# Reading the first 512 columns of an up projection in turns, and issuing compression products in pairs of groups

## The chip, the cores and the metric

The kernel runs on one core of a Trainium2 chip. The metric is device time of one execution in microseconds (us). Engines are named as the profile names them: PE is TensorE (products), PEld its weight loads, DVE is VectorE, ACT is ScalarE, POOL is GpSimd and SP is SyncE, whose queue issues nearly all loads.

## The reference

One layer of a hybrid decoder, for 256 tokens of width 2048, in float32. Cut to what matters here:

```python
def compress_blocks(k, pe, w1, w2):        # keys and values of attention's compressed branch
    ...                                    # 15 overlapping blocks of 32 tokens, each 32*128 long
    return jax.nn.gelu(flat @ w1) @ w2     # w1: 4096 x 256, once for keys, once for values

def conv_ffn(h, w_up, conv_w, conv_b, w_down):
    a, g = jnp.split(h @ w_up, 2, axis=-1) # w_up: 2048 x 11264
    a = causal_dwconv(a, conv_w, conv_b)
    return (jax.nn.silu(a) * g) @ w_down

# per layer
mod = (c_act @ w_ada[l] + b_ada[l])        # w_ada: 2048 x 12288, six vectors
h = layer_norm(x) * (1.0 + sc1) + sh1
y = token_mixer(h, w_in[l], ...)           # w_in: attention, mLSTM and merge gates
x = layer_norm(ALPHA * x + g1 * y, ...)
h = layer_norm(x) * (1.0 + sc2) + sh2
y = conv_ffn(h, w_up[l], ...)
x = layer_norm(ALPHA * x + g2 * y, ...)
```

## The kernel before

**Precision.** Most products are made in the reduced type fp32r (the profile writes f32 for it too). A weight tile `w` is split into a high part `wh` (a cast on ScalarE, L147) and a low part `wl` (a subtraction on VectorE, L150), and the activations likewise; three products (high-high, high-low, low-high) stand for one float32 product. A few small products stay native float32: these show as two instructions (passes) each.

**Reading in turns.** Where weights are the moving operand, `turns` (L111) lets the product read its columns as two halves alternately: column 0, column 256, column 1, column 257 and so on. The host has put the even columns into the first half and the odd ones into the second (`_even_odd`), so that the result has its old order. All projections with moving weights do so, but the first 512 columns of the up projection.

**Loading.** `load` (L121) takes a buffer of the pool `w` (seven of 512 KB) and issues a load on SP's queue, in the order of the program. `load_split` (L141) splits the tile; `wh` and `wl` have four buffers each. A `w` buffer comes free when its tile is split, or, for a tile that is used as it is, when its products are done.

**The input projection and the compression.** The input projection runs over three groups of k tiles. In the last group it goes through 21 tiles of `w_in_b` (products `ps_b`, 256 columns), then 14 of `w_in_a` (`ps_a`, 392 columns, four column blocks of 3.5 tiles), then 7 of `w_in_v`. `stream` calls `work()` once for every such tile. `work()` normally ticks the ticker `tk`, which at rate 1.0 issues one half row of `w_ada` (a 512 KB load and, one tick later, a VectorE product, L269). The compression starts when the thirteenth of the 21 `w_in_b` tiles has been gone through; it is a generator, and while it lasts `work()` only moves it on:

```python
if comp and next(comp[0], 1) is None:
    return
comp.clear()
```

`compress` (L593) makes for the keys, then for the values: `xe` (the blocks with their position term, L599 and L604; one buffer for both), eight groups of products `ps_hid` (L611), and behind them a copy `hp` (L616), four small products `ps_hs` (L619) and a Gelu. One group loads one 512 KB tile of `cmp_w1` and makes four native products of 32 columns by 256, in four column strips of the array. The scheduler places them on TensorE where they are ready.

**The first 512 columns of the up projection.** Columns 0 to 255 of both halves of `w_up` are handled apart, while the normalisation ahead of the feed-forward runs, in an order written out by hand (L1427 on, `manual_schedule`). Here the weights are the moving operand, 512 columns, into `acc` (`ps_u`). `turn2` transposes four k tiles of one half of the tokens (`ps_n`), `modulated` scales and shifts them, `high_part` and `low_part` split them into `h2T`. For the first half of the tokens and k tiles 0 to 11, `exact` (L1385) makes native products straight from the unsplit tile `raws`, 12 in all; `products` (L1415) makes the other 60 in fp32r from tiles that `early_split` has split. The results are transposed in `up(0)` and `up(1)`.

Of the kernel before, what the change touches and what calls it, by code (L numbers as in the profile page):

```python
# [14 lines left out]
P = 128  # L15
# [7 lines left out]
DFF = 5632  # L23
# [57 lines left out]
def build(ctx: ExitStack, tc: tile.TileContext, d, out, dbg=None):  # L81
# [26 lines left out]
    def mm(o, lhsT, rhs, start, stop):  # L108
        nc.tensor.matmul(o, lhsT, rhs, start=start, stop=stop)  # L109
# [483 lines left out]
    def compress():  # L593
        gTs = []
        w2t = t2([P, 2, 2, P], "w2t")
        nc.sync.dma_start(w2t, d["cmp_w2"].rearrange("p (a b c) -> p a b c", a=2, b=2))
        for kv in range(2):
            xe = pa.tile([P, 32, 2, 16], F32, name="xe", tag="xe")
            nc.gpsimd.memset(xe, 0.0)  # L599
            ch = accC[:, 2 * kv:2 * kv + 2, :].rearrange("p g (n q) -> p q g n", q=16)  # L600
            for a in range(2):
                pe = prm[:, R_PE + 32 * kv + 16 * a:R_PE + 32 * kv + 16 * a + 16]
                for g in range(2):
                    nc.vector.tensor_tensor(xe[:, 16 * a:16 * a + 16, g, 0:NCMP],  # L604
                                            ch[:, :, g, a:a + NCMP],
                                            pe[:, :, None].to_broadcast([P, 16, NCMP]), op=ALU.add)
            ps = bank(psa, "ps_hid")
            for i in range(8):
                t = load(d["cmp_w1"][kv * 8 + i])
                for l in range(4):  # L610
                    mm(ps[32 * l:32 * l + 32, :256],  # L611
                       xe[:, 4 * i + l, :, :].rearrange("p g n -> p (g n)"),
                       t[:, l * 256:(l + 1) * 256], i == 0, i == 7)
                yield
            hp = t2([P, 256], "hp")
            nc.vector.tensor_copy(hp, ps[:, :256])  # L616
            ps = bank(psa, "ps_hs")
            for ho in range(2):
                mm(ps[:, ho * 32:(ho + 1) * 32], hp[:, ho * P:(ho + 1) * P], sel4, True, True)  # L619
            if kv:  # L620
                gt = t2([P, 4, 3, 16], "gT1")
                nc.scalar.activation(gt, ps[:, :64].rearrange("p (a n) -> p a n", a=4)[:, :, None, :]
                                     .to_broadcast([P, 4, 3, 16]), AF.Gelu_apprx_tanh)
            else:
                gt = pa.tile([P, 2, 32], F32, name="gT0")
                nc.scalar.activation(gt, ps[:, :64].rearrange("p (a b) -> p a b", a=2), AF.Gelu_apprx_tanh)
            gTs.append(gt)
        ps = bank(psa, "ps_kc")
        for ho in range(2):
            mm(ps[:, :32], w2t[:, 0, ho, :], gTs[0][:, ho, :], ho == 0, ho == 1)  # L630
        nc.vector.tensor_copy(kcT[:, :, :16], ps[:, :32].rearrange("p (a b) -> p a b", a=2))
        ps = bank(psa, "ps_vc")
        for g in range(2):
            for ho in range(2):
                mm(ps[:48, g * P:(g + 1) * P],
                   gTs[1][:, 2 * ho + g].rearrange("p a n -> p (a n)"), w2t[:, 1, ho, :],
                   ho == 0, ho == 1)
        src = ps[:48, :2 * P].rearrange("p (a b) -> p a b", a=2)
        nc.scalar.copy(vcm, src)
        nc.vector.tensor_sub(vcm[32:48], src[32:48], vcm[32:48])  # L640
# [131 lines left out]
    for gi, kn in enumerate(GROUPS):  # L772
# [16 lines left out]
        c = 0  # L789
# [594 lines left out]

    def exact(q, t, i):  # L1385
        k = 4 * q + i
        mm(acc[t], tmps[q, t][:, i, :], raws[k // 2][:, k % 2 * 512:(k % 2 + 1) * 512], k == 0, False)

    def turn2(q, t):
        psn[q, t] = bank(psa, "ps_n2")  # L1390
# [23 lines left out]

    def products(q, t, lo, ks=range(4)):  # L1415
        for k in [4 * q + i for i in ks]:
            wh, wl = [w[:, k % 2 * 512:(k % 2 + 1) * 512] for w in ews[k // 2]]
            x = h2T[:, k, lo, t * P:(t + 1) * P]
            if lo:
                mm(acc[t], x, wh, False, k == KD - 1)  # L1420
            else:
                mm(acc[t], x, wh, k == 0, False)
                mm(acc[t], x, wl, False, False)
# [265 lines left out]
def pack(inputs):  # L1689
    import numpy as np  # L1690
    f = {k: np.asarray(v) for k, v in inputs.items()}
    r = {}
    r["x"] = np.ascontiguousarray(f["x"][0])

    i = np.arange(P)
    e = np.zeros((P, R_HEAD), np.float32)
    e[:, R_ID:R_ID + P] = np.eye(P)
    e[:, R_C:R_C + KD] = f["c"][0].reshape(KD, P).T
    e[:, R_BADA:R_BADA + 96] = f["b_ada"][0].reshape(96, P).T
    r["head"] = e  # L1700
    c = q = np.zeros((P, R_N), np.float32)
    c[:, C_U:C_U + P] = i[:, None] <= i[None, :]
    c[:, C_ONE:C_ONE + 8] = 1.0
    r["msk"] = np.where(i[None, :] > i[:, None], NEG, 0.0).astype(np.float32)
    n = np.arange(16)
    for t in range(2):
        ok = (CMP_STRIDE * n[None, :] + CMP_LEN - 1 <= (t * P + i)[:, None]) & (n[None, :] < NCMP)
        c[:, C_CADD + 16 * t:C_CADD + 16 * t + 16] = np.where(ok, 0.0, NEG)
        c[:, C_C01 + 16 * t:C_C01 + 16 * t + 16] = ok
    c[:, C_SEL:C_SEL + 32] = (i % 32)[:, None] == np.arange(32)[None, :]  # L1710
    q[:, R_CW:R_CW + 32] = f["ml_conv_w"][0].reshape(4, 8, P).transpose(2, 1, 0).reshape(P, 32)
    q[:, R_CB:R_CB + 8] = f["ml_conv_b"][0].reshape(8, P).T
    fc = np.zeros((P, R_FN), np.float32)
    fc[:, :R_FB] = f["ffn_conv_w"][0].reshape(3, KF, P).transpose(2, 1, 0).reshape(P, 3 * KF)
    fc[:, R_FB:] = f["ffn_conv_b"][0].reshape(KF, P).T
    r["ffn"] = fc
    q[:, R_PE:R_PE + 64] = f["cmp_pe"][0].transpose(2, 0, 1).reshape(P, 64)
    q[:, R_NG:R_NG + 8] = f["ml_norm_g"][0].reshape(8, P).T
    r["prm"] = q
    r["ml_gate_b"] = f["ml_gate_b"]  # L1720
    r["ln_g"] = f["ln_g"][0]
    r["ln_b"] = f["ln_b"][0]

    wa = np.ascontiguousarray(f["w_ada"][0].T).reshape(6 * KD, P, 2, 1024)
    r["w_ada"] = np.ascontiguousarray(wa.transpose(0, 2, 1, 3)).reshape(12 * KD, P, 1024)

    w = f["w_in"][0]
    kv = lambda br, k, g: w[:, 1024 + ((br * 2 + k) * 2 + g) * P:1024 + ((br * 2 + k) * 2 + g + 1) * P]
    bc = [kv(0, 0, 0), kv(0, 0, 1), kv(0, 1, 0), kv(0, 1, 1),
          kv(1, 0, 0), kv(2, 0, 0), kv(1, 0, 1), kv(2, 0, 1), w[:, :1024], w[:, 2584:3608]]  # L1730
    bc = np.concatenate(bc, 1)
    ac = np.concatenate([w[:, 4640:5664], w[:, 2560:2584], w[:, 4632:4640], kv(1, 1, 0), kv(1, 1, 1),
                         kv(2, 1, 0), kv(2, 1, 1), w[:, 3608:4632]], 1)
    tb, ta, tv = [], [], []
    k0 = 0
    for gi, kn in enumerate(GROUPS):
        rows = slice(k0 * P, (k0 + kn) * P)
        u = bc[rows].reshape(kn, P, NBLK, P)
        u = np.stack([u[k, :, b, :] for b, ks in order_b(gi) for k in ks]).reshape(-1, 8, P, P)
        tb.append(np.ascontiguousarray(u.transpose(0, 2, 1, 3)).reshape(-1, P, 1024))  # L1740
        ta.append(_pack_u(_even_odd(ac[rows, :A_MV], AW), AW, 2))
        tv.append(_pack_u(_even_odd(ac[rows, A_MV:], 512), 512, 2))
        k0 += kn
    r["w_in_b"] = np.concatenate(tb)
    r["w_in_a"] = np.concatenate(ta)
    r["w_in_v"] = np.concatenate(tv)
    mg = [_pack_a(_even_odd(m, 512), 512).reshape(4, 8, P, 1024) for m in (w[:, 5664:7712], w[:, 7712:])]
    r["w_mg"] = np.stack(mg, 1).reshape(64, P, 1024)
    br = [_pack_a(_even_odd(f[m][0], 512), 512).reshape(4, 4, P, 1024) for m in ("w_br_nsa", "w_br_ml")]
    r["w_br"] = np.stack(br, 1).reshape(32, P, 1024)  # L1750
    r["w_o"] = _pack_rows(f["w_o"][0])
    up = f["w_up"][0]
    r["w_up"] = np.stack([_pack_b(up[:, :DFF], 8), _pack_b(up[:, DFF:], 8)], 1).reshape(KF * 4, P, 1024)
    r["w_up"][:8] = _pack_a(np.concatenate([up[:, c:c + 2 * P] for c in (0, DFF)], 1), 512)
    dn = f["w_down"][0]
    r["w_down"] = np.concatenate([_pack_a(_even_odd(dn[:DFF // 2], 512), 512), _pack_rows(dn[DFF // 2:])])
    w1 = f["cmp_w1"][0].reshape(2, 8, 4, P, 256)
    r["cmp_w1"] = w1.transpose(0, 1, 3, 2, 4).reshape(16, P, 1024)
    r["cmp_w2"] = f["cmp_w2"][0].reshape(2, 2, P, P).transpose(2, 0, 1, 3).reshape(P, 512)
    return {k: np.ascontiguousarray(v) for k, v in r.items()}  # L1760
# [20 lines left out]
```

## Time and profile before

| What | us |
|---|---|
| Runs: median of 3 (lowest, highest) | 1375.86 (1375.83, 1376.8) |
| The profiled execution | 1377.45 |
| Its span, first to last instruction | 1375.4 |
| TensorE busy | 1356.4 |
| VectorE busy | 1089.1 |
| ScalarE busy | 733.5 |

Busy time is a union of overlapping instructions: a product's duration contains the filling of the pipeline, and the next one starts before it ends. The work that a product costs TensorE is read from the distance between two starts. In a timeline row the first number is the start and the second the time from the first instruction's start to the last one's end, both in us; x is how many instructions of one kind follow each other; the brackets at the end hold idle time before it and what ended it. The mean granted clock of TensorE over the span is 0.997.

### The profile page before, as it was taken

Reading aid. Unit: us, or ns where it says so; the run is one execution under the profiler, and the core shown is the slowest. Engines: PE = TensorE matmul, PEld = TensorE weight load, DVE = VectorE, ACT = ScalarE, POOL = GpSimd, SP = SyncE. Lnnn points to the kernel's source line nnn. Section 1 sums busy time; section 2 is a strip of 40 time slices with the busy share of each in tenths; the row PEclk is TensorE's granted clock in tenths of the full one; section 3 lists DMA queues with packets and bytes.
Section 4 is the critical chain, followed back from the end, with each engine's and each line's share of the span. In section 5 each row is a group of like instructions: output and inputs, shape, how many; then the busy total and the mean of one; then the engine's idle time right before and its main releaser. Section 6 shows DMA issues by size and latency. Waiting matters only on the chain.

```text
span 1375.4 us, 20986 instructions
## 1 busy us (share of the span) xinstructions
PE 1356.4 (99%) x7890; PEld 1208.5 (88%) x7890; DVE 1089.1 (79%) x1643; ACT 733.5 (53%) x1053; POOL 3.6 (0%) x11
## 2 busy tenths in 40 slices
PE   7999999999999999999999999999999999999998
PEld 6999998888778888889689999988889999998887
DVE  7899977888787998789889889855557676765568
ACT  6644455646576444445665565553445555555342
POOL 0000000000000000000000000000000000000000
PEclk9999999999999999999999999999999999999999
DMA  9999978996877999996389878866676666666662
GB/s 372 418 419 365 393 258 280 350 314 230 323 255 273 381 339 359 362 343 250 119 323 310 296 251 301 293 197 206 198 205 201 202 203 202 200 200 200 205 201 84
DMA packets 103302, 374.09 MB, mean 272 GB/s; under 512 B 11168, under 2 KB 11680, under 8 KB 102432
## 3 DMA queue, kind: packets, MB, share of 16 engines
q1 hardware_dynamic: 103200, 372.75, 78.0%
q8 instruction: 62, 1.02, 0.3%
q14 instruction: 40, 0.33, 0.1%
HBM read 370.61 MB, written 2.10 MB: 271 GB/s over the span
## 4 chain that ended last, share of the span: by engine, by line
PE 85%; DVE 8%; DMA 2%; issue 2%; ACT 2%; SPq 0%; DVEq 0%; ACTq 0%
PE ps_up L109 32%; PE ps_d L109 14%; PE ps_mg L109 12%; PE ps_b L109 7%; PE ps_br L109 6%; PE ps_a L109 5%; PE ps_o L109 3%; DVE wl L150 3%; PE ps_u L109 2%; DVE adaA L251 1%; DMA w<-in_w_in_b_dram 1%; PE ps_s L109 1%; PE ps_y L109 1%; DVE adaB L251 1%; PE ps_hid L109 1%
## 5 line engine op out<-in xcount | busy, mean ns | idle before, releaser
L150 DVE TENSOR_TENSOR wl<-w,wh 128x1024 fp32r<-128x1024 f32 (+1 forms) x470 | 564.3, 1205 | 248.3 <-ACT wh L147 245.0
L147 ACT CAST wh<-w 128x1024 fp32r<-128x1024 f32 (+1 forms) x470 | 484.4, 1035 | 513.2 <-PE ps_up L109 145.0
L109 PE MATMUL ps_up<-h2T,wh 128*128 128x512 f32 x1344 | 440.6, 382 | 0.0
L109 PE MATMUL ps_up<-h2T,wl 128*128 128x256 f32 x1344 | 366.3, 273 | 0.0
L109 PEld LDWEIGHTS ps_up<-h2T,wh 128*128 128x128 f32 x1344 | 253.9, 189 | 35.4
L109 PEld LDWEIGHTS ps_up<-h2T,wl 128*128 128x128 f32 x1344 | 258.0, 192 | 0.1
L109 PE MATMUL ps_d<-wh,uTt 128*128 128x512 f32 (+1 forms) x704 | 198.5, 366 | 0.0
L109 PE MATMUL ps_mg<-wh,hT 128*128 128x512 f32 x512 | 163.1, 389 | 0.0
L269 DVE SCALAR_TENSOR_TENSOR w<-w,crow 128x1024 f32<-128x1024 f32 x132 | 160.7, 1218 | 0.0
L109 PEld LDWEIGHTS ps_d<-wh,uTt 128*128 128x128 f32 x704 | 129.8, 189 | 16.5
L109 PE MATMUL ps_b<-hT,wh 128*128 128x256 f32 x768 | 125.8, 278 | 3.5 <-ACT hT L429 2.5
L109 PE MATMUL ps_d<-wl,uTt 128*128 128x512 f32 (+1 forms) x352 | 128.8, 366 | 0.0
L109 PEld LDWEIGHTS ps_b<-hT,wh 128*128 128x128 f32 x768 | 111.7, 193 | 7.4 <-ACT hT L429 3.2
L109 PEld LDWEIGHTS ps_mg<-wh,hT 128*128 128x128 f32 x512 | 96.8, 189 | 16.0 <-issue 3.1
L109 PE MATMUL ps_a<-wh,hT 128*128 128x392 f32 (+1 forms) x384 | 103.5, 348 | 0.0
L109 PE MATMUL ps_mg<-wl,hT 128*128 128x512 f32 x256 | 97.2, 380 | 0.0
L109 PE MATMUL ps_b<-hT,wl 128*128 128x256 f32 x384 | 91.5, 278 | 0.0
L109 PEld LDWEIGHTS ps_a<-wh,hT 128*128 128x128 f32 x384 | 69.4, 189 | 5.4 <-issue 2.2
L109 PEld LDWEIGHTS ps_d<-wl,uTt 128*128 128x128 f32 x352 | 66.7, 189 | 8.3
L109 PEld LDWEIGHTS ps_b<-hT,wl 128*128 128x128 f32 x384 | 68.4, 195 | 0.1
L109 PE MATMUL ps_a<-wl,hT 128*128 128x392 f32 (+1 forms) x192 | 67.0, 350 | 1.3 <-DVE wl L150 1.2
L109 PE MATMUL ps_o<-wh,mgT 128*128 128x512 f32 x192 | 57.4, 379 | 0.0
(323 smaller groups left out, 1414.7 us busy)
## 6 DMA issues: line engine op xcount, KB each, us to landing
w<-in_w_up_dram SPq DMA_DIRECT2D x176, 512.0 KB, 4.3
w<-in_w_ada_dram SPq DMA_DIRECT2D x132, 512.0 KB, 5.0
w<-in_w_down_dram SPq DMA_DIRECT2D x89, 512.0 KB, 4.2
w<-in_w_mg_dram SPq DMA_DIRECT2D x64, 512.0 KB, 5.1
w<-in_w_in_b_dram SPq DMA_DIRECT2D x48, 512.0 KB, 9.8
w<-in_w_br_dram SPq DMA_DIRECT2D x32, 512.0 KB, 5.3
w<-in_w_o_dram SPq DMA_DIRECT2D x32, 512.0 KB, 5.1
adaA<-in_w_ada_dram SPq DMA_DIRECT2D x15, 1024.0 KB, 10.2
```

The source lines that it names most:

```text
L109: nc.tensor.matmul(o, lhsT, rhs, start=start, stop=stop)
L147: hi = nc.scalar.copy(wh[:, :n], t[:, :n])
L150: lows.append(nc.vector.tensor_sub(wl[:, :n], t[:, :n], wh[:, :n]))
L251: ins = nc.vector.scalar_tensor_tensor(t, t, 1.0, crow, op0=ALU.mult, op1=ALU.mult, accum_out=parts[:, row(m), k, 0:1])
L269: ins = nc.vector.scalar_tensor_tensor(t, t, 1.0, crow[:, i * 1024:(i + 1) * 1024], op0=ALU.mult, op1=ALU.mult, accum_out=parts[:, row(m), ...
```

## The change

Three places. `compress` yields after every second group instead of after each, so that two groups are issued in a row and one call of `work()` moves it on by two. `exact` and `products` read their moving operand through `turns`. The host stores the first 512 columns (the first eight tiles of `w_up`) with even columns first, then odd ones.

```diff
@@ compress
                     mm(ps[32 * l:32 * l + 32, :256],
                        xe[:, 4 * i + l, :, :].rearrange("p g n -> p (g n)"),
                        t[:, l * 256:(l + 1) * 256], i == 0, i == 7)
-                yield
+                if i % 2:
+                    yield
@@ exact
-        mm(acc[t], tmps[q, t][:, i, :], raws[k // 2][:, k % 2 * 512:(k % 2 + 1) * 512], k == 0, False)
+        mm(acc[t], tmps[q, t][:, i, :], turns(raws[k // 2][:, k % 2 * 512:(k % 2 + 1) * 512]),
+           k == 0, False)
@@ products
-            wh, wl = [w[:, k % 2 * 512:(k % 2 + 1) * 512] for w in ews[k // 2]]
+            wh, wl = [turns(w[:, k % 2 * 512:(k % 2 + 1) * 512]) for w in ews[k // 2]]
@@ pack
-    r["w_up"][:8] = _pack_a(np.concatenate([up[:, c:c + 2 * P] for c in (0, DFF)], 1), 512)
+    r["w_up"][:8] = _pack_a(_even_odd(np.concatenate([up[:, c:c + 2 * P] for c in (0, DFF)], 1), 512), 512)
```

## The prediction

> **What bounds the kernel now.** I read the page first, then who waited for whom on TensorE, then busy time by stretch around the two edits, then single rows of the timelines.
>
> ```profile
> span 1375.4 us, 20986 instructions
> ```
>
> ```profile
> PE ps_a L109 <- DVE wl L150: 1.2, 3, 0.7
> ```
>
> All that TensorE waits for split weight tiles in the projections beside the compression is 1.2 us in three times (the columns: us in total, times, longest). What counts is then the distance from one product's start to the next, since durations overlap, and whether the next weight tile goes on being split in time. By stretch (columns: busy of PE, PEld, DVE, ACT, POOL, clock, DMA share, GB/s):
>
> ```profile
> 190.00:200.00 10.00, 10.00 (x95) 9.79 (x98) 7.19 (x11) 5.69 (x8) 0.00 (x0) 1.00 0.74 249
> 200.00:210.00 10.00, 10.00 (x104) 8.75 (x94) 7.08 (x10) 3.77 (x5) 0.00 (x0) 1.00 0.84 321
> 210.00:220.00 10.00, 10.00 (x96) 8.46 (x95) 8.17 (x15) 6.93 (x12) 0.00 (x0) 1.00 0.89 299
> 220.00:230.00 10.00, 10.00 (x75) 9.47 (x74) 9.92 (x20) 4.78 (x9) 0.96 (x1) 1.00 0.68 212
> 230.00:240.00 10.00, 10.00 (x94) 7.42 (x94) 4.19 (x7) 4.67 (x7) 0.00 (x0) 1.00 0.80 284
> 240.00:250.00 10.00, 10.00 (x72) 9.04 (x65) 7.15 (x12) 3.79 (x5) 0.41 (x1) 1.00 0.99 379
> 250.00:260.00 10.00, 10.00 (x72) 8.77 (x71) 7.85 (x16) 8.79 (x12) 0.00 (x0) 1.00 0.98 368
> ```
>
> From 190 to 250 us, where the compression runs, TensorE has full clock and no gap; DMA and VectorE have room until 240, none and little after it.
>
> **Part 1, compression products two groups in a row.** No instruction is added or removed. One group is four native products of 32 columns, eight passes. TensorE's timeline, first a run of three, then a single group:
>
> ```profile
> 199.43 0.28 PE L109 MATMUL ps_b<-hT,wl 128*128 128x256 f32 x1
> 199.64 1.50 PE L109 MATMUL ps_hid<-w,xe 128*32 128x256 f32 x24
> 201.07 0.49 PE L109 MATMUL ps_b<-hT,wh 128*128 128x256 f32 x2
> 201.40 0.28 PE L109 MATMUL ps_b<-hT,wl 128*128 128x256 f32 x1
> ```
>
> ```profile
> 206.42 0.28 PE L109 MATMUL ps_b<-hT,wl 128*128 128x256 f32 x1
> 206.63 0.64 PE L109 MATMUL ps_hid<-w,xe 128*32 128x256 f32 x8
> 207.19 0.49 PE L109 MATMUL ps_b<-hT,wh 128*128 128x256 f32 x2
> 207.52 0.28 PE L109 MATMUL ps_b<-hT,wl 128*128 128x256 f32 x1
> 207.63 0.39 PE L109 MATMUL ps_b<-hT,wh 128*128 128x256 f32 x2
> ```
>
> Undisturbed products of 256 columns start 0.11 us apart (207.52 to 207.63). The single group pushes the third product behind it to 207.52 where 206.42 + 0.33 = 206.75 would do: 0.77 us. The run of three costs 201.40 - 199.43 - 0.33 = 1.64 us. So a further group in a run costs (1.64 - 0.77) / 2 = 0.435 us, and each change into and out of the 32-column form 0.77 - 0.435 = 0.335 us. The runs of before begin at 199.64, 206.63, 210.07, 213.51, 216.96 and 220.40 for the keys, and 230.85 (four groups), 234.24, 236.99, 239.75 and 242.50 for the values: 11 runs. The first two stand above; the first and the last of the values' five:
>
> ```profile
> 230.85 1.93 PE L109 MATMUL ps_hid<-w,xe 128*32 128x256 f32 x32
> ...
> 242.50 0.64 PE L109 MATMUL ps_hid<-w,xe 128*32 128x256 f32 x8
> ```
>
> After it, eight pairs. The two first runs were already long since xe came late; late again, it joins two pairs each time, which leaves three runs for each half, 6 in all (bounds: 8 with no joining, 4 if all is late). Gain 5 x 0.335 = **1.7 us**, between 1.0 and 2.3, as long as TensorE stays fed.
>
> What the pairs move is the larger question. work() calls the generator once for each weight tile and skips the ticks while it lasts. Half the yields end it eight tiles earlier: all sixteen groups now lie beside the eight last w_in_b tiles, and the eleven a tiles of columns 0 to 2 each bring one 512 KB w_ada load and its VectorE product, where three did. On SP's queue each of the eight last w_in_b loads stands behind two cmp_w1 loads instead of one, in the same seven w buffers, which cmp_w1 tiles hold until their group has run. Cost, by row:
>
> ```profile
> 20.00:100.00 80.00, 76.27 (x587) 73.75 (x587) 70.22 (x73) 48.09 (x73) 0.00 (x0) 0.98 1.03 419
> 214.39 0.97 DVE L150 TENSOR_TENSOR wl<-w,wh 128x784 fp32r<-128x784 f32 x1 [1.13 <-ACT wh L147]
> 223.75 0.33 PE L109 MATMUL ps_a<-wh,hT 128*128 128x392 f32 x1
> 231.55 1.28 ACT L626 ACT_TABLE_LOAD   x1
> 245.06 0.98 DVE L150 TENSOR_TENSOR wl<-w,wh 128x784 fp32r<-128x784 f32 x1 [1.59 <-ACT wh L147]
> 245.95 1.22 DVE L269 SCALAR_TENSOR_TENSOR w<-w,crow 128x1024 f32<-128x1024 f32 x1
> 246.99 0.49 PE L109 MATMUL ps_a<-wh,hT 128*128 128x392 f32 x2
> ```
>
> - DMA: eight 512 KB loads come forward into 190 to 250 us, 8 x 1.25 = 10.0 us at 419 GB/s or 11.1 at 379. The six stretches leave 10 x (0.26 + 0.16 + 0.11 + 0.32 + 0.20 + 0.01) = 10.6 us idle. It fits, barely, if all of it can be used.
> - VectorE: 8 x 1.2 = 9.6 us more, against 60 - 43.7 = 16.3 us idle there. It fits.
> - The lead of the splits over TensorE: the first a tile is split at 215.36 and used at 223.75, 8.4 us later; the tenth, counted by splits of 784 columns (245.06 to 246.04), is used at 247.16, the second product of the row at 246.99: 1.1 us. An a tile takes 12 products of 0.166 us, 2.0 us, while it and a w_ada tile (0.926 MB) need 2.4 us at 379 GB/s.
> - ScalarE: the keys' Gelu now falls among the convolution's Silu, one or two more table loads of 1.28 us; ScalarE is at most 69% busy there, and the splits' lead hides them (without it, 1.3 us once).
>
> If tiles come when they came, TensorE arrives 1.7 us sooner at a tile that was 1.1 us ahead, and waits 0.6 us. Bounds: 0, when the idle DMA time is all used, and 5.8 us (rival A). I take **0.6 us**, as the stretch from 250 to 260 us runs at a DMA share of 0.98 with w_ada loads in it, and TensorE does not stop there.
>
> Later the w_ada queue ends some eight loads sooner; nothing on TensorE waits for it there, so no gain.
>
> **Part 2, the first 512 columns.** 60 products in fp32r and 12 native ones (24 passes) read their 512 columns as two halves in turns; the permutation is on the host. Contiguous against turned:
>
> ```profile
> L109 PE MATMUL ps_u<-w,hm x24: 592/592/697, 666.2 to 677.5; 128*128 128x512 f32 x24
> 669.30 6.17 PE L109 MATMUL ps_u<-w,hm 128*128 128x512 f32 x14
> 675.95 1.50 ACT L1404 ACTIVATE hm<-ps_n,modc 128x128 f32<-128x128 f32 x4 [1.06 <-PE ps_n L1393]
> 680.75 1.37 DVE L1402 TENSOR_SCALAR hm<-ps_n,modc 128x128 f32<-128x128 f32 x4 [0.87 <-PE ps_n L1393]
> 686.80 1.22 DVE L150 TENSOR_TENSOR wl<-w,wh 128x1024 fp32r<-128x1024 f32 x1
> 688.07 0.50 PE L109 MATMUL ps_u<-wl,h2T 128*128 128x512 f32 x1
> 688.40 0.39 PE L109 MATMUL ps_u<-wh,h2T 128*128 128x512 f32 x1
> ...
> 691.39 0.39 PE L109 MATMUL ps_u<-wl,h2T 128*128 128x512 f32 x1
> ```
>
> ```profile
> 1000.42 0.38 PE L109 MATMUL ps_d<-wl,uTt 128*128 128x512 f32 x1
> ...
> 1003.66 0.38 PE L109 MATMUL ps_d<-wl,uTt 128*128 128x512 f32 x1
> ```
>
> 13 steps from 688.40 to 691.39 are 0.230 us each; the down projection's turned products make 15 steps in 3.24 us, 0.216. So 0.014 us each, 0.84 us for 60. Not all shows: the product at 688.07 starts when VectorE has finished wl (686.80 + 1.22 = 688.02). VectorE is then in one unbroken row from 680.75, which began with the transposes behind the first eight products. Of the 36 before 688 I count those eight, 0.11 us; the 24 after it count in full, 0.34. Together **0.45 us**; bounds 0.34 and 0.84.
>
> The native passes start (6.17 - 0.592) / 13 = 0.429 us apart, twice the turned fp32r step for as many columns, so the reading isn't what they wait for: 0 gained. No row shows a native product reading in turns. Its bounds are -0.36 us (24 x 0.015, what fp32r gains) and +10.3 us (every pass doubled). I take 0, as a turned read already feeds 512 columns in 0.216 us. [...]
>
> **Sum.** -1.7 + 0.6 - 0.45 = -1.55 us. The profiled execution took 1377.45 us (span 1375.4 and 2.05 around it), which would become 1375.9. It stands 1.6 us above the median of the runs, 1375.86; from the median, **1374.3 us**, 0.11% less. What a measurement of this kernel can tell from no change is about 0.2%, 2.75 us, so I forecast no difference that can be told.
>
> **Rivals.**
> A. The a tiles starve (slower). Place: the fifth to the eleventh a tile. Mechanism: cmp_w1 tiles fill the w buffers while xe is rebuilt for the values, and SP stands still behind them, as 220 to 230 us shows (share 0.68); then a tile and w_ada load in turns give a tile every 2.4 us where 2.0 is wanted. If half of the 10.6 us idle stays idle, 5.2 us of the 10.5 don't fit; with 1.1 us of lead and TensorE 1.7 us earlier, the wait is 5.2 - 1.1 + 1.7 = 5.8 us: 1375.86 - 2.15 + 5.8 = 1379.5. The time passes that of before once over 1.5 us don't fit, and is slower by over 0.2% from 4.3 us on. Against it: 1.1 us of lead at the worst tile, and 8.4 us of lead at the first. Chance 0.18.
> B. Everything comes in: four runs, 60 steps, no waiting: -2.3 - 0.84 = -3.1, 1372.7. Against it are the wait at 688.07 and the lead of 1.1. Chance 0.17 that it reaches 2.75.
> C. The grouping does little: pairs aren't joined, 8 runs, and what is saved is waited for later: -1.0 + 0.6 - 0.45, 1375.0. No change that can be told. Chance 0.15.
> D. Native products slow down when read in turns. These 24 passes lie on the chain (ScalarE stood idle 1.06 us until the transposes behind them, row at 675.95), so all of it shows; it cancels the rest from 1.55 / 24 = 0.065 us a pass on, and at half a pass, 0.215, the time is 1375.86 - 1.55 + 5.2 = 1379.5. Chance 0.04. [...]
>
> The forecast itself has 0.46. Faster by over 0.2%: 0.17 (B). Slower: 0.20 (most of A, D). Same: the forecast, C and the rest, 0.63. The range is from B's 1372.7 to 1379.0, short of A's and D's ends; the likeliest case alone lies within 1373.5 and 1375.2.
>
> **What would show it.** ps_hid in six runs on TensorE, none a single group of 8, the last before the first ps_a product; ps_u steps of 0.216 in fp32r and 0.429 native; w_ada loads beside every a tile. Wrong: waits of ps_a for wl summing over 3 us, or ps_u<-w,hm durations above 592.

## The result, and the profile after

The changed kernel is slower: 1383.88 us median of six runs (1381.85 to 1384.95), beside 1376.76 of the kernel before on the same chip (1375.83 to 1378.92, six runs). The ratio is 1.0051, 95% interval 1.0041 to 1.006. The profiled execution took 1384.77 us. Both parts of the change cost time, each in a place that the prediction had named as a rival.

Three views of the changed kernel show it. First the span and who waited for whom on TensorE (us in total, times, longest us):

```profile
span 1383.0 us, 20993 instructions
```

```profile
PE ps_a L109 <- DVE wl L150: 3.8, 7, 0.9
...
PE ps_a L109 <- ACT wh L147: 1.4, 2, 1.0
```

5.2 us in nine waits for split tiles over the whole span. Four of them, 1.5 us, lie ahead of 190 us; so do the three of before, 1.2 us, of which none lies beside the compression. The other five, 3.6 us, are new and stand between 241 and 265 us. By stretch, in the columns that the prediction named (busy time of PE, PEld, DVE, ACT, POOL, clock, DMA share, GB/s):

```profile
240.00:250.00 10.00, 8.56 (x50) 7.80 (x49) 9.97 (x16) 3.92 (x6) 0.00 (x0) 1.00 0.95 319
250.00:260.00 10.00, 9.06 (x54) 8.47 (x53) 8.81 (x17) 6.76 (x8) 0.00 (x0) 1.00 1.02 401
260.00:270.00 10.00, 8.79 (x46) 7.52 (x45) 8.10 (x14) 8.09 (x10) 0.00 (x0) 1.00 0.88 313
```

TensorE, without a gap there before, is now idle for 3.6 us in these three stretches. In the first two VectorE and the DMA queues are close to full.

Where the time goes, read from single tiles: each row gives the least, median and longest duration in ns, then the first and the last start in us. First the kernel before, then the changed one:

```profile
L109 PE MATMUL ps_hid<-w,xe x128: 379/379/403, 199.6 to 242.8; 128*32 128x256 f32 x128
L109 PE MATMUL ps_mg<-wl,hT x256: 378/379/462, 280.0 to 566.5; 128*128 128x512 f32 x128
L109 PE MATMUL ps_u<-wh,h2T x40: 387/390/497, 678.2 to 693.4; 128*128 128x512 f32 x40
```

```profile
L109 PE MATMUL ps_hid<-w,xe x128: 379/379/403, 198.5 to 226.4; 128*32 128x256 f32 x128
L109 PE MATMUL ps_mg<-wl,hT x256: 378/379/463, 284.1 to 570.6; 128*128 128x512 f32 x128
L109 PE MATMUL ps_u<-w,hm x24: 701/703/1122, 671.0 to 685.4; 128*128 128x512 f32 x24
L109 PE MATMUL ps_u<-wh,h2T x40: 379/379/562, 685.8 to 700.7; 128*128 128x512 f32 x40
```

From the first compression product to the first mixing gate (ps_mg) it took 280.0 - 199.6 = 80.4 us, and now 284.1 - 198.5 = 85.6: 5.2 us more. Three ps_b products that stood ahead of the first compression product now stand behind it (172 of them against 169), 0.3 us, so that 4.9 us are lost. The compression is over 16 us sooner. The mixing gates take as long as before. From the first to the last native ps_u product it took 11.3 us (the row of before stands in the prediction) and now 14.4: 3.1 lost. From there to the last fp32r product of wh it took 15.9, and now 15.3: 0.6 won.

The native passes by their timeline, the run of 14 that took 6.17 us before, with the transposes ahead of it:

```profile
669.26 1.92 PE L1395 MATMUL ps_n<-head,n 128*128 128x128 f32 x8 [1.90 <-ACT n L1373]
670.97 4.11 PE L109 MATMUL ps_u<-w,hm 128*128 128x512 f32 x6
674.92 0.60 PE L1395 MATMUL ps_n<-head,n 128*128 128x128 f32 x4
675.36 7.72 PE L109 MATMUL ps_u<-w,hm 128*128 128x512 f32 x14
```

(7.72 - 0.703) / 13 = 0.540 us a pass, where a pass read straight took 0.429: 0.111 more, times 23 steps 2.6 us. The other 0.5 us of the 3.1 are in the six passes from 670.97, where TensorE's granted clock was halved for a while:

```profile
669.36:672.78 3.42, 3.42 (x11) 2.24 (x12) 3.30 (x7) 2.97 (x8) 0.00 (x0) 0.50 0.00 0
```

And what VectorE does while TensorE waits for the a tiles, one row per run of instructions:

```profile
241.40 0.96 DVE L150 TENSOR_TENSOR wl<-w,wh 128x784 fp32r<-128x784 f32 x1
242.28 1.22 DVE L269 SCALAR_TENSOR_TENSOR w<-w,crow 128x1024 f32<-128x1024 f32 x1
243.43 0.09 DVE L269 DVE_READ_ACCUMULATOR w<-w,crow 128x1 f32 x1
243.43 0.97 DVE L150 TENSOR_TENSOR wl<-w,wh 128x784 fp32r<-128x784 f32 x1
...
247.49 1.04 DVE L863 TENSOR_TENSOR projA<-ps_a,projA 128x392 f32<-128x392 f32 x2
...
255.67 0.97 DVE L150 TENSOR_TENSOR wl<-w,wh 128x784 fp32r<-128x784 f32 x1
```

Split, w_ada product, split, w_ada product, an addition to projA after some three tiles, VectorE busy for 14.17 of 14.27 us: six tiles from 241.40 to 255.67, 2.38 us a tile. TensorE needs 12 x 0.166 = 2.0 us for one. That looks like a bound by VectorE; the experiments had to tell it from one by the DMA queue, which was the prediction's rival A.

The last of the five waits, 1.0 us at 264 us, ends with a cast on ScalarE instead. ScalarE had no idle time ahead of it: the gates' activations with three table loads (1.28 us each) stood there from 256.10 on, with one cast among them. The last of them and the cast:

```profile
261.72 1.28 ACT L687 ACT_TABLE_LOAD   x1
...
263.13 2.92 ACT L147 CAST wh<-w 128x1024 fp32r<-128x1024 f32 x3
```

In the kernel before, the same activations run with three table loads, but the first tile of this kind (1024 columns) is split by 258.19 and used from 260.62 on, and TensorE does not wait. No run changes this one alone.

### The profile page after: what moved, and what is told of

The parts are those of the page before. It is cut to its first block, busy times and chain, and to the rows that moved or that the text cites. A ratio compares the mean times of both kernels' runs of the same rounds, so it can differ in the third digit from the quotient of the medians.

```text
span 1383.0 us, 20993 instructions
## 1 busy us (share of the span) xinstructions
PE 1359.8 (98%) x7890; PEld 1209.3 (87%) x7890; DVE 1089.4 (79%) x1643; ACT 737.0 (53%) x1055; POOL 3.6 (0%) x11
## 4 chain that ended last, share of the span: by engine, by line
PE 82%; DVE 9%; DMA 4%; issue 2%; ACT 2%; SPq 0%; DVEq 0%; ACTq 0%
PE ps_up L109 32%; PE ps_d L109 14%; PE ps_mg L109 12%; PE ps_br L109 6%; PE ps_b L109 6%; PE ps_a L109 4%; PE ps_o L109 3%; DVE wl L150 3%; PE ps_u L109 2%; DMA w<-in_w_in_a_dram 1%; DMA w<-in_w_o_dram 1%; PE ps_s L109 1%; PE ps_y L109 1%; DMA w<-in_w_in_b_dram 1%; ACT wh L147 1%
## 5 line engine op out<-in xcount | busy, mean ns | idle before, releaser
L109 PE MATMUL ps_d<-wh,uTt 128*128 128x512 f32 (+1 forms) x704 | 198.5, 366 | 0.0
```

## The experiments

The kernel before was run again beside each set of experiments. Its median is 1377.21 us for the second part alone, the first part alone, the w_ada tiles held back and straight native reading; 1376.88 for products in pairs with loads one by one and the two kernels built on it; 1376.74 for short products, short loads, the lowered rate and the changed kernel once more. Ratios have their 95% interval.

**The second part alone** (`exact` and `products` in turns, `compress` as before).

> The kernel before with the second edit alone (the first 512 columns of the up projection read in turns, native and fp32r products), compression as before. Theory: the 24 native passes start 0.540 us apart instead of 0.429, 24 x 0.111 = 2.7 us, and the fp32r products give back 0.45 us: slower by 2.2 us, 1378.1 from a median of 1375.86; ps_u<-w,hm durations above 700 as in the changed kernel. Rival: the native passes are slow in the changed kernel only because TensorE's granted clock fell to 0.5 from 669 to 673 us in its profile; then, without that drop, they are at 592 again and the time is 0.45 us below before.

Measured: 1378.89 us, ratio 1.0014 (1.0005 to 1.0023), 1.7 us more than before. Its native products:

```profile
L109 PE MATMUL ps_u<-w,hm x24: 701/703/802, 665.2 to 679.0; 128*128 128x512 f32 x24
L109 PE MATMUL ps_u<-wh,h2T x40: 379/379/562, 679.3 to 694.3; 128*128 128x512 f32 x40
```

13.8 us for the native stretch instead of 11.3, 2.5 more, and 15.3 for the fp32r stretch instead of 15.9. TensorE's granted clock is 1.00 there, from 664 to 685 us, so the rival falls: the slow passes belong to the reading. +2.5 - 0.6 is 1.9, near the 1.7 measured.

**The first part alone** (the edit in `compress`).

> The kernel before with the first edit alone (compression products two groups in a row), the up projection as before. Theory: the a tiles starve: TensorE waits for split weights between 240 and 262 us, and every milestone from the mixing gates on is 4.1 us later; slower by 4.1 us, 1380.0, with 10 runs of compression products. Rival: the up projection's loads and the late stages share in the loss, so that the pairs alone cost under 2 us.

Measured: 1380.84 us, ratio 1.003 (1.0018 to 1.0042), 3.6 us more. Waits and milestones:

```profile
PE ps_a L109 <- DVE wl L150: 3.4, 6, 0.8
...
PE ps_a L109 <- ACT wh L147: 1.7, 2, 1.0
```

```profile
L109 PE MATMUL ps_mg<-wl,hT x256: 378/379/462, 283.9 to 570.5; 128*128 128x512 f32 x128
```

The loss stands there whole before the mixing gates begin (283.9 - 198.5 = 85.4 us from the first compression product, for 80.4), and the rival (a share lost in late stages) falls. About 1.2 us of it comes back at the last layer norm, where TensorE waited 0.5 us for `n` (the normalised rows) instead of 1.7; the changed kernel's first profile waited 1.9.

**The first part, with the w_ada tiles held back.**

```diff
         def work():
             if comp and next(comp[0], 1) is None:
                 return
+            if comp:
+                held_back[0] = 9
             comp.clear()
+            held_back[0] -= 1
+            if held_back[0] > 0:
+                return
```

> The kernel before with the first edit alone, but after the compression has ended the eight next calls bring no w_ada tile, so that the w_ada loads stand where they stood in the kernel before. Theory one (a w_ada load beside every a tile takes the DMA time that the a tiles need): the waits of ps_a go back to about 1 us, and the time is that of before less one change of form, 1375.5. Theory two (the compression's loads, two by two in front of each w_in_b load, eat the lead before the a tiles begin): the waits of ps_a stay above 3 us, and the time is 2 to 4 us above before, 1378 to 1380.

Measured: 1376.73 us, ratio 0.9995 (0.9986 to 1.0004). The waits are those of before, none of them beside the a tiles:

```profile
PE ps_a L109 <- DVE wl L150: 1.2, 3, 0.7
```

Theory two falls. The loads of the compression two by two do no harm; it is the w_ada work, brought forward to stand beside every a tile.

**Is it VectorE or the DMA queue?** Two kernels, each the first part alone, ease one of the two for the w_ada tiles beside the a tiles (`beside` is true from the end of the compression to the end of the third column block; the lines that set it are left out here). Neither computes the gates in full.

```diff
-            def products(t=t, i=i):
+            def products(t=t, i=i, n=128 if beside[0] else 1024):
                 ins = nc.vector.scalar_tensor_tensor(
-                    t, t, 1.0, crow[:, i * 1024:(i + 1) * 1024], ...
+                    t[:, :n], t[:, :n], 1.0, crow[:, i * 1024:i * 1024 + n], ...
```

> Pairs alone, and the VectorE products of the w_ada tiles that come beside the a tiles take 128 of their 1024 columns (the sums over the rest are left out, so the gates are not computed in full); their loads stay whole. Theory one (VectorE sets the pace: per three a tiles three splits, three w_ada products and the additions to projA, 7.1 us against the 6.0 us that TensorE needs): the products fall from 1.22 to about 0.2 us, VectorE keeps up, the waits of ps_a go back to about 1 us and the loss of 4.1 us goes, to about before or a little below it, 1375 to 1376. Theory two (the DMA queue sets it, a load of 512 KB and one of 392 KB per a tile): the waits stay above 3 us and the time at 1379 to 1381.

```diff
+            n = 64 if beside[0] else 1024
-            t = load(d["w_ada"][(m * KD + k) * 2 + i])
+            t = load(d["w_ada"][(m * KD + k) * 2 + i][:, :n])
...
+                if n < 1024:
+                    a, cr = [x[:, :1024][:, n:].rearrange("p (r n) -> p r n", n=n) for x in (t, cr)]
+                    b = t[:, :n][:, None, :].to_broadcast([P, 15, n])
...
```

> Pairs alone, and of the w_ada tiles that come beside the a tiles only 64 of 1024 columns are loaded (32 KB instead of 512); their VectorE products run over the 64 columns 15 times, so that VectorE works as long as before (the gates are not computed from the right numbers). Theory one (VectorE sets the pace): nothing changes, waits of ps_a above 3 us and 1379 to 1381. Theory two (the DMA queue sets it): the waits go and the time is about that of before.

Measured: short products 1380.58 us, ratio 1.003 (1.0019 to 1.0041); short loads 1379.01, ratio 1.0013 (1.0004 to 1.0022). Neither theory holds alone. The stretch from 230 to 260 us, first with short products, then with short loads:

```profile
230.00:260.00 30.00, 28.03 (x171) 24.75 (x170) 19.16 (x51) 18.44 (x25) 0.00 (x0) 1.00 0.96 348
```

```profile
230.00:260.00 30.00, 29.03 (x184) 26.80 (x182) 29.91 (x51) 15.30 (x21) 0.00 (x0) 1.00 0.68 203
```

With short products VectorE is free for 10.8 of 30 us and the DMA queues stay at a share of 0.96. The splits now wait for ScalarE's casts (the bracket), and four of the casts between 241 and 254 us for loads of `w_in_a`, 5.8 us in all. The first of these casts, then the first and the last of six splits:

```profile
242.65 0.84 ACT L147 CAST wh<-w 128x784 fp32r<-128x784 f32 x1 [1.33 <-DMA w<-in_w_in_a_dram]
```

```profile
241.36 0.98 DVE L150 TENSOR_TENSOR wl<-w,wh 128x784 fp32r<-128x784 f32 x1 [0.83 <-ACT wh L147]
...
254.29 0.96 DVE L150 TENSOR_TENSOR wl<-w,wh 128x784 fp32r<-128x784 f32 x1
```

That is five tiles in 12.9 us, 2.6 us each; 0.926 MB at 348 GB/s are 2.7 us. With short loads the DMA share falls to 0.68 and VectorE has no idle time left, 29.91 of 30; seven tiles from 242.20 to 258.34 take it 2.3 us each. So both are short at nearly the same height, 2.3 us and 2.6 us a tile against TensorE's 2.0, and easing one finds the other. By the medians, easing the loads gave back 1.4 of the 3.6 us (the two intervals overlap) and easing VectorE nothing.

**Both eased, with every w_ada product kept**: the first part alone, and the ticker's rate beside the a tiles lowered.

```diff
-GR1, GR2 = 1.0, 0.5
+GR1, GR2 = 0.6, 0.5
```

> Pairs alone, the planner's rate beside the a tiles at 0.6 instead of 1.0, so that six or seven of the eleven a tiles bring a w_ada tile; the rest comes later, in the mixing gates. Theory one: per three a tiles VectorE has 1.8 products in place of 3, 5.6 us, under TensorE's 6.0: most of the loss goes, within 0.5 us of before, with waits of ps_a of 1 to 2 us. Rival: any w_ada load beside the a tiles costs its share, 0.6 of the 4.1 us stay, 1378.3.

Measured: 1376.81 us, ratio 1.0000 (0.9992 to 1.0009).

```profile
PE ps_a L109 <- DVE wl L150: 1.2, 3, 0.7
```

By the times the whole loss is gone with eight w_ada products instead of eleven between 229 and 260 us, and TensorE has no idle time left beside the a tiles (busy for 30.00 of the 30 us from 230 on); the rival, a share for every load, falls.

The time of a kernel also holds the wait for `n` at the last layer norm, which differs between these profiles and, for the changed kernel, between two of its executions. So compare the stage itself, from the first ps_hid to the first ps_mg<-wl of each profile:

| Profile | stage, us | wait for `n`, us |
|---|---|---|
| before | 80.4 | 1.68 |
| changed | 85.6 | 1.90 |
| first part alone | 85.4 | 0.49 |
| short products | 84.6 | 1.40 |
| short loads | 82.9 | 0.66 |
| lowered rate | 81.6 | 0.48 |
| w_ada tiles held back | 80.0 | 2.69 |

In the stage, easing VectorE gave back 0.8 us and easing the loads 2.5; with the tiles held back the whole loss is gone. With the lowered rate 1.2 us remain without any idle time: 0.3 are the three ps_b products, and the small attention products `ps_sT` come in three runs instead of one, two more changes, which at 0.335 us each would be 0.7 of the 0.9 left; that is an estimate, as no run shows the price of a change for these products. The shorter wait for `n` covers this in its profile.

**Products in pairs, loads one by one.** The compression's weights are loaded with each call, as before; two groups' products are issued on every second call. TensorE then has 8 runs of compression products where before had 11.

```diff
+            pair = []
             for i in range(8):
-                t = load(d["cmp_w1"][kv * 8 + i])
-                for l in range(4):
-                    mm(...)
+                pair.append((i, load(d["cmp_w1"][kv * 8 + i])))
+                while i % 2 and pair:
+                    n, t = pair.pop(0)
+                    for l in range(4):
+                        mm(...)
                 yield
```

> The up projection as before; the compression's weights come one tile with each call as before, so that its loads and the w_ada loads stand where they stood, but its products are issued for two groups on every second call: 8 runs of compression products where before had 11. Theory (the loss of the first edit is all in the loads it moves, and a change of form costs 0.335 us): 3 x 0.335 = 1.0 us less than before, 1374.9 from 1375.86, waits of ps_a for split weights at about 1 to 2 us. Rival: the products in pairs disturb the supply themselves (tiles are held twice as long), and the time is that of before or above it.

Measured: 1375.86 us, ratio 0.9992 (0.9983 to 1.0001): 1.0 us less by the medians, the size expected, but not told from no change. In the profile it is plain:

```profile
L109 PE MATMUL ps_hid<-w,xe x128: 379/379/403, 200.3 to 242.5; 128*32 128x256 f32 x128
```

42.2 us from the first compression product to the last, where before took 43.2; up to the mixing gates it is 79.4 us for 80.4. Three runs fewer, 1.0 us: the 0.335 us for each change of form stands.

**Straight native reading, fp32r reading in turns where the layout allows it.**

```diff
@@ products
+            if t:
+                wh, wl = turns(wh), turns(wl)
@@ up(0): copy out of the first bank
-    nc.scalar.copy(ub[0], acc[0])
+    nc.scalar.copy(ub[0].rearrange("p (b a) -> p b a", a=2), turns(acc[0]))
@@ host
-    r["w_up"][:8] = _pack_a(np.concatenate(...), 512)
+    r["w_up"][:8] = _pack_a(_even_odd(np.concatenate(...), 512), 512)
```

> Compression as before; of the first 512 columns the native products and the fp32r products of the first 128 rows read straight, those of the second 128 rows read in turns (the weights lie with even and odd columns apart, and the copy out of the first bank puts them in order). Theory: ps_u<-w,hm at 592 again, the turned fp32r steps at 0.2155: the time is 0.2 to 0.5 us below before, 1375.4 to 1375.7, no difference that can be told. Rival: the copy out of the bank in turns, or the mixing of two layouts, costs more than the products give, and the time is 0.5 us or more above before.

Measured: 1376.47 us, ratio 0.9996 (0.9987 to 1.0005). No difference that can be told, as expected; the native passes are at a median of 592 ns again.

**These two together, and with four groups in a row** (`i % 4 == 3` for `i % 2`).

> Products in pairs with the loads left one by one, together with straight native reading and turned fp32r reading for the second 128 rows alone. Theory: the two gains add, 1.0 + 0.4 = 1.4 us below before (ratio 0.9990). Rival: as TensorE comes 1 us sooner it waits for the a tiles, and less than 0.7 us remain.

> As the one before, with the products of four groups issued together on every fourth call: 5 runs of compression products. Theory: 6 x 0.335 + 0.4 = 2.4 us below before (ratio 0.9982). Rival: four weight tiles of the compression stand in the seven buffers at a time, the w_in_b and a tiles come later, and TensorE waits more than the 1 us that is gained over pairs.

Measured: 1376.82 us, ratio 0.9995 (0.9986 to 1.0003), and 1377.3, ratio 1.0006 (0.9997 to 1.0015). The first is unclear: its profile has both gains, its runs spread from 1374.12 to 1377.94. The second can't be told from it by time; its profile shows the rival:

```profile
L109 PE MATMUL ps_hid<-w,xe x128: 379/379/403, 198.5 to 239.7; 128*32 128x256 f32 x128
```

```profile
250.00:260.00 10.00, 8.61 (x60) 6.92 (x60) 8.05 (x15) 9.82 (x13) 0.00 (x0) 1.00 1.01 396
```

41.2 us for the compression, 2.0 less than before (six changes of form, as reckoned), and 1.4 us of idle TensorE in the ten us from 250 on, at a DMA share of 1.01. No version beats the kernel before by more than can be told.

**Native reading by itself.**

```diff
+    "straight": ap,
+    "one":       ap.rearrange("p (a b) -> p b a", a=2),
+    "two":       ap.rearrange("p (a b c) -> p b a c", a=2, c=2),   # "four", "thirtytwo": c=4, c=32
+    "quarters":  ap.rearrange("p (a b) -> p b a", a=4),
+    "stride":    ap.rearrange("p (b a) -> p a b", a=2),
```

> A kernel that computes nothing of the reference: only products of 512 columns into full banks, 12 native and 24 fp32r ones for each way of reading the moving tile (straight; two halves in turns by 1, 2, 4 and 32 elements; four quarters in turns; every second element), each way twice. [...] Theory two (native pays for any pattern of two dimensions): turns by 2, 4 and 32 elements as slow as by one. Theory three (in the kernel the native passes lose the time to something else there, a transfer or a weight load): 0.43 in all of them.

Measured, in the second round (24 instructions a row; the step is the distance to the next row's start, divided by 24; r is fp32r, n native):

```profile
148.08 11.41 PE L55 MATMUL ps_r_stride<-wh,xh 128*128 128x512 f32 x24
159.32 6.97 PE L55 MATMUL ps_r_quarters<-wh,xh 128*128 128x512 f32 x24
166.12 5.83 PE L55 MATMUL ps_r_thirtytwo<-wh,xh 128*128 128x512 f32 x24
171.79 6.17 PE L55 MATMUL ps_r_four<-wh,xh 128*128 128x512 f32 x24
177.80 8.32 PE L55 MATMUL ps_r_two<-wh,xh 128*128 128x512 f32 x24
185.94 5.35 PE L55 MATMUL ps_r_one<-wh,xh 128*128 128x512 f32 x24
191.13 5.62 PE L55 MATMUL ps_r_straight<-wh,xh 128*128 128x512 f32 x24
196.60 10.96 PE L55 MATMUL ps_n_stride<-w,xt 128*128 128x512 f32 x24
207.40 21.11 PE L55 MATMUL ps_n_quarters<-w,xt 128*128 128x512 f32 x24
228.34 10.48 PE L55 MATMUL ps_n_thirtytwo<-w,xt 128*128 128x512 f32 x24
238.65 10.46 PE L55 MATMUL ps_n_four<-w,xt 128*128 128x512 f32 x24
248.95 11.04 PE L55 MATMUL ps_n_two<-w,xt 128*128 128x512 f32 x24
259.83 13.12 PE L55 MATMUL ps_n_one<-w,xt 128*128 128x512 f32 x24
272.79 10.46 PE L55 MATMUL ps_n_straight<-w,xt 128*128 128x512 f32 x24
```

| us per step | straight | turns by 1 | by 2 | by 4 | by 32 | quarters | every second |
|---|---|---|---|---|---|---|---|
| native pass | 0.430 (first round) | 0.540 | 0.453 | 0.429 | 0.430 | 0.873 | 0.450 |
| fp32r product | 0.228 | 0.216 | 0.339 | 0.250 | 0.236 | 0.283 | 0.468 |

The native products read straight started at 61.99 in the first round and the next row at 72.31, (72.31 - 61.99) / 24 = 0.430 us. For native passes turns by one cost 0.110 us a pass, turns by two 0.023, turns by four or 32 elements nothing, and quarters double it. So theory two falls (0.453, 0.429 and 0.430 are not as slow as 0.540), and theory three too, as 0.540 stands here outside the kernel. The fp32r products have another order: only turns by one are at or under 0.216; turns by two are slower than straight by half (0.339 for 0.228).

**The changed kernel once more.**

> The changed kernel once more, for a second profile. If the fall of TensorE's clock to 0.5 at the last layer norm belongs to this kernel, it stands there again, with the wait of 1.9 us and the native passes up to 1122 ns; if it comes and goes from execution to execution, the steps before it (a tiles plus 4.1, native passes 0.540 us apart) stay and this one does not, and the execution is 0.6 us shorter there.

Measured: 1383.06 us, ratio 1.005 (1.0037 to 1.0062). Its profile:

```profile
669.14 1.36 PE L1395 MATMUL ps_n<-head,n 128*128 128x128 f32 x8 [0.49 <-ACT n L1373]
670.35 3.51 PE L109 MATMUL ps_u<-w,hm 128*128 128x512 f32 x6
...
674.13 7.72 PE L109 MATMUL ps_u<-w,hm 128*128 128x512 f32 x14
```

The fall of the clock is not there, the passes of 0.540 us are. So the fall comes and goes. In this profile the a tiles cost 4.8 us (285.3 - 199.8 - 80.4, by its starts of ps_mg and ps_hid, less the 0.3 of the three ps_b products), the wait for `n` gives back 1.2 (0.49 for 1.68), the native passes cost 2.6 and the fp32r products give 0.6: 5.6 us. In the first profile, without the 1.2 and with the clock's fall, the same sum is 4.9 + 0.7 + 3.1 - 0.6 = 8.1, the 0.7 being the longer wait for `n` (0.2) and the slow transposes behind it (0.5). (The span of that profile is 7.6 us longer than before's: its last group of k tiles began 0.8 us sooner, ahead of both edits, and 0.3 us came at the end.) The medians, 7.1 and 6.3 us above before, lie between the two sums. The two parts alone make 1.7 + 3.6 = 5.3; that the remaining 1 to 2 us are the wait and the clock is argued from these two profiles, not shown by a run that holds them fixed.

## Why the prediction was wrong

- **The bound of the kernel and the places** were read rightly: what moved lies in the two stretches named and in the wait for `n` just ahead of the second, which the prediction had not named. One reading was wrong: the 1.2 us of waits for split tiles do not lie beside the compression but ahead of 190 us.
- **Six runs of compression products: wrong.** There were ten. That a late `xe` joins two pairs did not happen, and the values' half broke into single groups. Of the 1.7 us one change of form was saved, 0.3. The price of a change, 0.335 us, was right (8 runs gave 1.0 us, 5 runs 2.0).
- **The supply wait, 0.6 us: the step that failed first.** It measured 5.2 us up to the mixing gates (the 4.9 lost there and the 0.3 that the form saved), near the upper bound of 5.8 that stood as rival A with a chance of 0.18. The two sentences "It fits, barely" and "It fits" compared sums over the six stretches. The idle DMA and VectorE time lay mostly before 240 us, ahead of the tiles that needed it. The prediction had the right comparison in its own third bullet, 2.4 us of loading against 2.0 us of products for a tile, and did not carry it over the tiles. It never made that comparison for VectorE: 0.89 for a split, 1.14 for a w_ada product and the projA additions are 2.38 a tile. So rival A had the place and the size, and half of the mechanism: with the loads eased half of the loss in the stage stays, since VectorE stands right behind (busy for 29.91 of 30 us there); and the compression's own loads, which rival A began with, do no harm by themselves (80.0 us for the stage with the w_ada tiles held back, 80.4 before). The lead of the splits, which was to hide ScalarE's table loads, was used up too: one wait of 1.0 us ends with ScalarE.
- **fp32r in turns, 0.45 us: right**, measured 0.6 in three profiles, steps of 0.216.
- **Native in turns, 0: the other step that failed.** The argument, that a turned fp32r read feeds 512 columns in 0.216 us and a pass has twice that, took two kinds of product for one. It measured +0.111 a pass, 2.6 us, inside the bounds given (-0.36 to +10.3), and was rival D with a chance of 0.04. The native passes of the probe take 0.540 us with one element from a half in turn, 0.453 with two, 0.429 with four and 0.430 straight; the fp32r products are fastest with one in turn, 0.216. The prediction took the fp32r row for both. What the native passes lose the time to in such a reading, no run shows.
- **The signs it named for itself** came true on the bad side: waits of ps_a on wl of 3.8 us (over 3; 1.2 of them stood before), native durations of 703 (above 592).

With all four terms as measured, the sum is -0.3 + 5.2 - 0.6 + 2.6, 6.9 us, where -1.55 was forecast; the wait at the layer norm and the clock move it by about 1 either way. 7.1 was measured.

## What to carry to other kernels

Room that is counted over a stretch says little when the work that comes forward lands on one part of it: compare the pace per tile there, for each engine and for the queue, with what the consumer needs, and multiply the difference by the tiles. Where two suppliers are short at nearly the same height (here 2.3 and 2.6 us a tile), easing one shows only the other, so test them one by one and then together. A reading order that is free for one type of product has to be measured for the other before it is applied (here 0.216 us for 0.228 in fp32r, but 0.540 for 0.430 native).

## What the runs showed of the hardware

- A native product pays for reading two halves in turns by one element (0.540 us a pass of 512 columns against 0.430), and takes twice as long for four quarters in turns (0.873). fp32r products have another order altogether: 0.216 in turns by one, 0.228 straight, 0.339 by two, 0.250 by four. Why two are worse than one and than four, no run shows.
- TensorE's granted clock fell to 0.50 for 3.42 us in the middle of a busy stream, after a wait of 1.90 us, in the changed kernel's first profile, and again for 3.41 us in the kernel with the w_ada tiles held back after one of 2.69 us, where the native products then took 13.0 us instead of 11.3. The second fall:

```profile
666.09:669.50 3.41, 3.41 (x5) 1.35 (x5) 3.31 (x9) 3.07 (x9) 0.00 (x0) 0.50 0.00 0
```

It did not after 1.68 us at the same place in the kernel before (1.00 from 664 to 685 us), nor after 0.49 in the changed kernel's second profile (1.00 from 663 to 685 us). What brings the fall on, no run shows. Part of the spread between executions of one kernel may come from this; no run here settles how much.
